# One encoder layer with SSD and windowed attention on one core: the order of work in the SSD forward pass

## The chip, the cores and the metric

The kernel runs on one core of a Trainium2 chip. The metric is the device time of one execution in microseconds. Engines are named TensorE (PE in the rows; PEld is its weight load), VectorE (DVE), ScalarE (ACT), GpSimd (POOL) and SyncE (SP, which here only issues DMAs). Each executes its own queue in order; semaphores hold an instruction until what it reads has been produced.

## The reference

One layer on x of 1024 tokens by 1024 features: RMS norm, one input projection, then two branches. Branch A is a bidirectional state-space scan (SSD) with 16 heads in 2 groups; branch B is windowed attention. Both are gated and normed, concatenated, projected, added to x, and normed. The part that the change touches, for one direction, chunks of 128 tokens:

```python
X = (xh * dt[..., None]).reshape(b, c, CHUNK, SSM_GROUPS, SSM_HPG, SSM_HEAD_DIM)
cs = jnp.cumsum(a, axis=-1)
L = jnp.exp(jnp.where(tril, cs[..., :, None] - cs[..., None, :], -jnp.inf))
CB = jnp.einsum('bclgn,bcsgn->bgcls', Cc, Bc)
y_diag = jnp.einsum('bghcls,bcsghp->bclghp', CB[:, :, None] * L, X)
states = jnp.einsum('bcsgn,bghcs,bcsghp->cbghpn', Bc, jnp.exp(cs[..., -1:] - cs), X)
# carried over the chunks: state = decay * state + states[c]
y_off = jnp.einsum('bclgn,cbghpn,bghcl->bclghp', Cc, states_in, jnp.exp(cs))
...
y = y_fwd + y_bwd + d_skip * xh
y_ssd = rms_norm(y * silu(z), ssd_norm_g)      # per group
```

## The kernel before

All products run on TensorE in 32-bit float; the large projections split each operand into a high and a low part (hi, lo) and take three products. The kernel has these stages: norm of x and transposes; convolution blocks of group 0; the SSD stage of group 0 (backward pass, then forward pass); convolutions of group 1; the SSD stage of group 1; attention, with the output projection fed in between; the rest of the output projection.

Each SSD pass is a loop over 8 chunks. Between its pieces `fill(n)` traces n halves of a projection block, 24 matmuls of 128x512 each (L146), which need nothing from the SSD work. A scheduler orders each engine's queue at build time by a model of the times, so work that was traced later can be placed earlier where its inputs are there.

In a chunk c of a group:

- `weighted(c, d)` (L540): GpSimd makes xd = xk * wst, ScalarE its rounded part xh (L545), VectorE the rest xl (L546).
- `advance(Sold, c, d)` (L549): three TensorE products of Bk with xh, xl, xh into a bank "s" (L552); GpSimd scales the old state by the decay (L557); VectorE adds the two (L558).
- `y_off` (L562): the carried state times CT (L570), times et from DRAM on VectorE (L572).
- Backward pass (L575): `y_off` into yo, which GpSimd's DMA adds to yb_d in DRAM (L579), `advance`, `fill(1)`.
- `scores(c)` (L587): loads cb[0] and cb[1] (E and F: the cumulative sums, broadcast, 512 KB each); TensorE product BT x CT (L596) into a bank "t", VectorE multiplies it by two masks into CB (L600). ScalarE adds the bias of each of 8 heads to E (L607), VectorE that of all heads to F (L608), takes the minimum (L609); ScalarE makes M from CB (L612) and exp(E) (L613); VectorE makes CB * dt in F (L614), adds (L616) and multiplies (L617). M is traced one chunk ahead.
- Forward pass (L621): `y_off` into yb, which a DMA issued by GpSimd accumulates with yb_d (L630); `fill`; the diagonal product of xk and M into the one bank "y" (L635); VectorE adds it to yb (L637); `advance`; then the gating: zt is loaded, GpSimd multiplies (yg, L643), SP's DMA stores yg to y_d (L644), ScalarE squares (L646), GpSimd adds parts (L647, L649) into sqs, which `add_sums` (L514) sums by TensorE (L519).

Buffers in the pool sp are 2 per tag where nothing else is said; xh and xl have 1, yo and yb share 3. PSUM has 3 banks "mm", 2 "t", 2 "s", 1 "y".

Of the kernel before, what the change touches and what calls it, by code (L numbers as in the profile page):

```python
# [10 lines left out]
F32 = mybir.dt.float32  # L11
# [5 lines left out]
P = 128  # L17
S = 1024
# [17 lines left out]
def kernel(  # L36
# [430 lines left out]
    def fill(n):  # L467
        while n:
            if next(left) is None:
                n -= 1  # L470
# [4 lines left out]
    def hb(t, d, c, g):  # L475
        return t[:, d, c, g * HPG:(g + 1) * HPG]

    def bc(t, n):
        return t.unsqueeze(2).broadcast_to([P, HPG, n])

    def v3(t):
        return t.rearrange("p (h d) -> p h d", h=HPG)
# [40 lines left out]
    for g in range(NG):  # L523
# [12 lines left out]
        if g == NG - 1:  # L536
            cpc.close()
            kv_pools.append(pool(ctx, "kvp", side="left"))

        def weighted(c, d):  # L540
            xd = sp.tile([P, 512], F32, tag="xd", name="xd")
            G.tensor_tensor(out=v3(xd), in0=v3(xk[:, c, :]), in1=bc(hb(wst, d, c, g), 64), op=ALU.mult)
            xh = sp.tile([P, 512], F32R, tag="xh", name="xh", bufs=1)
            xl = sp.tile([P, 512], F32R, tag="xl", name="xl", bufs=1)
            A.activation(out=xh, in_=xd, func=AF.Copy)  # L545
            V.tensor_tensor(out=xl, in0=xd, in1=xh.bitcast(F32), op=ALU.subtract)  # L546
            return xh, xl, xh

        def advance(Sold, c, d):  # L549
            ps = bank("s")  # L550
            for i, (b, x) in enumerate(zip((Bk[0], Bk[0], Bk[1]), weighted(c, d))):
                T.matmul(ps, lhsT=b[:, c, :], rhs=x, start=i == 0, stop=i == 2)  # L552
            Sn = sp.tile([P, 512], F32, tag="S", name=f"S{d}")
            if Sold is None:
                A.activation(out=Sn, in_=ps, func=AF.Copy)
            else:
                G.tensor_tensor(out=v3(Sn), in0=v3(Sold), in1=bc(hb(dec, d, c, g), 64), op=ALU.mult)  # L557
                V.tensor_tensor(out=Sn, in0=Sn, in1=ps, op=ALU.add)  # L558
            return Sn

# [14 lines left out]
        for c in range(NSB - 1, -1, -1):  # L575
            if Sb is not None:
                yo = sp.tile([P, 512], F32, tag="yo", name="yo", bufs=3)
                y_off(Sb, c, 1, yo)
                G.dma_start(out=yb_d[g, c], in_=yo, accum_op=ALU.add)  # L579
            if c > 0:  # L580
                Sb = advance(Sb, c, 1)
            if c == 5 and sums:
                add_sums()
            fill(1)
        Sf = None

        def scores(c):  # L587
            cb = []
            for d in range(2):
                t = sp.tile([P, HPG, P], F32, tag=f"cb{d}", name=f"cb{d}", bufs=2)  # L590
                r = cs_d[d, c * NH + g * HPG:c * NH + (g + 1) * HPG, :]
                nc.sync.dma_start(out=t.rearrange("p h l -> p (h l)"),
                                  in_=bass.AP(tensor=r.tensor, offset=r.offset, ap=[[0, P], [1, HPG * P]]))
                cb.append(t)
            ps = bank("t")
            T.matmul(ps[:, 0:P], lhsT=BT[:, c * P:(c + 1) * P], rhs=CT[:, c * P:(c + 1) * P],  # L596
                     start=True, stop=True)
            CB = sp.tile([P, 2, P], F32, tag="CB", name="CB")
            for d in range(2):
                V.tensor_tensor(out=CB[:, d, :], in0=ps[:, 0:P], in1=msk[:, d, :], op=ALU.mult)  # L600


            E, F = cb
            M = sp.tile([P, HPG, P], F32, tag="M", name="M")
            for h in range(HPG):
                hh = g * HPG + h
                A.activation(out=E[:, h, :], in_=E[:, h, :], func=AF.Identity, bias=ncs[:, 0, c, hh:hh + 1])  # L607
            V.tensor_tensor(out=F, in0=F, in1=bc(hb(ncs, 1, c, g), P), op=ALU.add)  # L608
            V.tensor_tensor(out=E, in0=E, in1=F, op=ALU.min)  # L609
            for h in range(HPG):  # L610
                hh = g * HPG + h
                A.activation(out=M[:, h, :], in_=CB[:, 0, :], func=AF.Copy, scale=dt[:, 0, c, hh:hh + 1])  # L612
            A.activation(out=E, in_=E, func=AF.Exp)  # L613
            V.tensor_tensor(out=F, in0=CB[:, 1, :].unsqueeze(1).broadcast_to([P, HPG, P]),  # L614
                            in1=bc(hb(dt, 1, c, g), P), op=ALU.mult)
            V.tensor_tensor(out=M, in0=M, in1=F, op=ALU.add)  # L616
            V.tensor_tensor(out=M, in0=M, in1=E, op=ALU.mult)  # L617
            return M

        Mn = scores(0)  # L620
        for c in range(NSB):  # L621
            M = Mn
            if c < NSB - 1:
                Mn = scores(c + 1)
            yb = sp.tile([P, 512], F32, tag="yo", name="yb", bufs=3)
            if Sf is None:
                nc.sync.dma_start(out=yb, in_=yb_d[g, c])
            else:
                y_off(Sf, c, 0, yb)
                G.dma_start(out=yb, in_=yb_d[g, c], accum_op=ALU.add)  # L630
            fill(FORWARD[c][0])
            py = bank("y")
            for h in range(HPG):
                a = h % 2 * 64
                T.matmul(py[a:a + 64, h // 2 * P:(h // 2 + 1) * P], lhsT=xk[:, c, h * 64:(h + 1) * 64],  # L635
                         rhs=M[:, h, :], start=True, stop=True)
            V.tensor_tensor(out=yb, in0=py, in1=yb, op=ALU.add)  # L637
            if c < NSB - 1:
                Sf = advance(Sf, c, 0)
            zt = sp.tile([P, 4, P], F32, tag="zt", name="zt", bufs=1)  # L640
            nc.sync.dma_start(out=zt, in_=z_d[g * 4:(g + 1) * 4, :, c * P:(c + 1) * P].rearrange("b p s -> p b s"))
            yg = sp.tile([P, 512], F32, tag="yg", name="yg", bufs=1)
            G.tensor_tensor(out=yg, in0=yb, in1=zt.rearrange("p b s -> p (b s)"), op=ALU.mult)  # L643
            nc.sync.dma_start(out=y_d[g, c], in_=yg)  # L644
            y2 = sp.tile([P, 512], F32, tag="y2", name="y2", bufs=1)
            A.activation(out=y2, in_=yg, func=AF.Square)  # L646
            G.tensor_tensor(out=y2[:, 0:256], in0=y2[:, 0:256], in1=y2[:, 256:512], op=ALU.add)  # L647
            sqs = sp.tile([P, P], F32, tag="sqs", name="sqs", bufs=6)
            G.tensor_tensor(out=sqs, in0=y2[:, 0:P], in1=y2[:, P:256], op=ALU.add)  # L649
            sums.append((g, c, sqs))  # L650
            if c == 5:
                add_sums()
            if g == NG - 1 and c == 4:
                load_kv(0, 0)
                load_q(0, 0)
                load_q(0, 1)
            fill(FORWARD[c][1])
    add_sums()
    ssd.close()

# [400 lines left out]
```

## Time and profile before

| | |
|---|---|
| median of 3 runs | 908.02 us (901.15 to 909.67) |
| profiled execution, its own time | 900.58 us |
| its span, first to last instruction | 898.8 us |
| TensorE busy | 848.2 us (94%) |
| VectorE busy | 569.2 us (63%) |
| ScalarE busy | 491.3 us (55%) |
| GpSimd busy | 356.6 us (40%) |
| mean granted TensorE clock | 0.989 |
| mean DMA traffic | 172 GB/s |

Busy time is the time in which an instruction of that engine was under way. Matmuls are pipelined, so their durations overlap; the time of a run of them is read from the starts. The SSD stage of group 0 lies at about 147 to 289 us of the span, that of group 1 at about 407 to 538 us.

### The profile page before, as it was taken

What the parts mean: (1) busy time and instruction counts of PE and PEld (TensorE: products, weight loads), DVE (VectorE), ACT (ScalarE), POOL (GpSimd) and SP (SyncE); (2) the same over time, 40 slices, a digit from 0 to 9 for tenths busy, and PEclk for the clock granted to TensorE, in tenths of its full rate; (3) what the DMA queues carried; (4) which work ended last, traced back from release to release, by engine and by line L of the source; (5) the groups of instructions that cost most, each with busy time, mean ns of one, the idle gap of its engine ahead of it and who ended that gap; (6) DMA issues with size and microseconds to landing.
All of it is one profiled execution on the core that took longest, in us unless ns stands there. A gap on an engine that the chain in (4) does not pass through costs nothing. (4 is left out here: it accounts for less than half of the span.)

```text
span 898.8 us, 13352 instructions
## 1 busy us (share of the span) xinstructions
PE 848.2 (94%) x4622; PEld 714.6 (80%) x4622; DVE 569.2 (63%) x971; ACT 491.3 (55%) x1118; POOL 356.6 (40%) x327
## 2 busy tenths in 40 slices
PE   3999999998898999999979999999999999899997
PEld 2999788886677888888857787887888888688786
DVE  4575766596898375446769945655766767555433
ACT  4642474353656345523645725788867866764222
POOL 3300012533865201134358552273653741735622
PEclk9999999999999999999998999999999999999999
DMA  8122473576788513477859869869856757424421
GB/s 296 75 83 59 155 222 128 141 222 187 223 234 256 166 47 94 117 206 177 261 131 253 225 190 246 243 200 308 245 149 182 221 131 190 145 56 136 132 87 47
DMA packets 127408, 154.25 MB, mean 172 GB/s; under 512 B 42331, under 2 KB 79899, under 8 KB 127212
## 3 DMA queue, kind: packets, MB, share of 16 engines
q1 hardware_dynamic: 121420, 141.35, 51.4%
q0 software_dynamic: 5776, 11.79, 7.4%
q8 instruction: 36, 0.59, 0.3%
q14 instruction: 32, 0.26, 0.1%
q10 hardware_dynamic: 144, 0.26, 0.1%
HBM read 111.58 MB, written 43.88 MB: 173 GB/s over the span
## 5 line engine op out<-in xcount | busy, mean ns | idle before, releaser
L146 PE MATMUL mm<-hhi,whi 128*128 128x512 f32 (+1 forms) x640 | 247.2, 389 | 1.8 <-ACT hhi L224 1.8
L146 PE MATMUL mm<-hlo,whi 128*128 128x512 f32 (+1 forms) x640 | 246.9, 387 | 0.0
L146 PE MATMUL mm<-hhi,wlo 128*128 128x512 f32 (+1 forms) x640 | 246.5, 386 | 0.0
L146 PEld LDWEIGHTS mm<-hhi,whi 128*128 128x128 f32 x640 | 121.6, 191 | 23.5 <-ACT hhi L224 2.5
L146 PEld LDWEIGHTS mm<-hlo,whi 128*128 128x128 f32 x640 | 121.9, 191 | 22.5 <-issue 1.7
L146 PEld LDWEIGHTS mm<-hhi,wlo 128*128 128x128 f32 x640 | 121.9, 191 | 21.7 <-issue 0.7
L695 PE MATMUL mm<-hhi,yl 128*128 128x512 f32 (+1 forms) x264 | 104.8, 397 | 0.8 <-POOL yl L687 0.8
L695 PE MATMUL mm<-hhi,yh 128*128 128x512 f32 (+1 forms) x264 | 104.7, 397 | 0.0
L695 PE MATMUL mm<-hlo,yh 128*128 128x512 f32 (+1 forms) x264 | 104.6, 396 | 0.0
L880 DVE CUSTOM_DVE_ANT_0 lg<-s,bias,nsnk 128x320 f32<-128x320 f32 (+2 forms) x128 | 64.6, 521 | 43.5 <-PE s L877 42.6
L883 ACT ACTIVATE lg<-lg,nm 128x320 f32<-128x320 f32 (+2 forms) x128 | 68.5, 535 | 18.3 <-DVE nm L880 16.4
L250 DVE SCALAR_TENSOR_TENSOR acc<-pad,prm_sb,acc 128x1024 f32<-128x1024 f32 x48 | 62.1, 1301 | 24.4 <-ACT acc L247 23.1
L687 POOL TENSOR_TENSOR yl<-y,yh 128x512 fp32r<-128x512 f32 x32 | 41.8, 1306 | 82.6 <-ACT yh L686 63.8
L134 ACT ACTIVATE whi<-wraw 128x1024 fp32r<-128x1024 f32 x38 | 40.0, 1054 | 41.9 <-PE mm L146 38.1
L137 POOL TENSOR_TENSOR wlo<-wraw,whi 128x1024 fp32r<-128x1024 f32 x12 | 30.2, 2518 | 69.0 <-ACT whi L134 69.0
L695 PEld LDWEIGHTS mm<-hhi,yl 128*128 128x128 f32 x264 | 50.2, 190 | 7.0 <-POOL yl L687 1.2
L607 ACT ACTIVATE cb<-cb,ncs 128x128 f32<-128x128 f32 x128 | 39.4, 390 | 29.8 <-DMA cb<-cs_d 29.8
L695 PEld LDWEIGHTS mm<-hhi,yh 128*128 128x128 f32 x264 | 50.3, 190 | 5.6
L695 PEld LDWEIGHTS mm<-hlo,yh 128*128 128x128 f32 x264 | 50.1, 190 | 5.5
L897 DVE TENSOR_TENSOR pl<-t,ph 128x512 fp32r<-128x512 f32 (+1 forms) x64 | 40.6, 654 | 18.7 <-ACT ph L896 18.0
L435 POOL TENSOR_TENSOR hlo<-oraw,hhi 128x512 fp32r<-128x512 f32 x32 | 41.0, 1292 | 26.6 <-ACT hhi L434 24.7
L137 DVE TENSOR_TENSOR wlo<-wraw,whi 128x1024 fp32r<-128x1024 f32 x26 | 33.7, 1297 | 24.0 <-ACT whi L134 21.4
(233 smaller groups left out, 1749.8 us busy)
## 6 DMA issues: line engine op xcount, KB each, us to landing
wraw<-in_w_blk_dram SPq DMA_DIRECT2D x38, 512.0 KB, 4.2
cb<-cs_d SPq DMA_DIRECT2D x32, 512.0 KB, 5.8
qt<-q_d SPq DMA_DIRECT2D x32, 256.0 KB, 3.8
oraw<-in_w_out_dram SPq DMA_DIRECT2D x32, 256.0 KB, 4.0
et<-es_d SPq DMA_DIRECT2D x56, 128.0 KB, 4.9
yb_d<-pad SPq DMA_DIRECT2D x8, 512.0 KB, 3.9
z_d<-gz SPq DMA_DIRECT2D x16, 256.0 KB, 3.8
zt<-z_d SPq DMA_DIRECT2D x16, 256.0 KB, 3.7
```

The source lines that it names most:

```text
L134: A.activation(out=hi, in_=raw, func=AF.Copy)
L137: eng.tensor_tensor(out=lo, in0=raw, in1=hi.bitcast(F32), op=ALU.subtract)
L146: yield T.matmul(ps, lhsT=l[:, kb, :], rhs=r[sh][:, kb, cols], start=(n == 0), stop=(n == 3 * NKB - 1))
L250: V.scalar_tensor_tensor(out=acc, in0=pad[:, k:k + S], scalar=cw[:, blk * 6 + k:blk * 6 + k + 1], in1=acc, op0=ALU.mult, op1=ALU.add)
L435: G.tensor_tensor(out=lo[:, c:c + 512], in0=raw, in1=hi[:, c:c + 512].bitcast(F32), op=ALU.subtract)
L607: A.activation(out=E[:, h, :], in_=E[:, h, :], func=AF.Identity, bias=ncs[:, 0, c, hh:hh + 1])
L687: G.tensor_tensor(out=lo, in0=t, in1=hi.bitcast(F32), op=ALU.subtract)
L695: yield T.matmul(ps[:, cols], lhsT=l[:, j * P:(j + 1) * P], rhs=r[:, dh * 512 + cols.start:dh * 512 + cols.stop], start=first and n == 0, ...
L880: V.tensor_tensor_reduce(out=l, in0=ps[:, d0 - c0:d1 - c0], in1=bias[:, hp, d0 - f0:d1 - f0], scale=-1.0, scalar=nsnk[:, sk], op0=ALU.add, ...
L883: A.activation(out=l, in_=l, func=AF.Exp, scale=-1.0, bias=nm, accum_out=sm)
L897: V.tensor_tensor(out=pl[0:w, 0:n], in0=ps[0:w, 0:n], in1=ph[0:w, 0:n].bitcast(F32), op=ALU.subtract)
```

## The change

In the SSD stage:

- GpSimd's instructions of a group are chained in the order in which they are traced (`ordered`), its accumulating DMAs among them. Splits of projection weights on GpSimd are not in the chain.
- xd has 1 buffer, xh and xl 2.
- In `advance` the scaling of the old state is traced ahead of the product, and the weighted x can be handed in.
- CB stays in PSUM, in columns 128 to 383 of the bank that holds its product.
- The bias of F is added by ScalarE, one instruction per head.
- In the forward pass `advance` stands ahead of the diagonal product, with xw of the chunk made in the previous one. The accumulating DMA stands behind the addition of the diagonal product. The gating (`finish`, `reduce`) is that of the previous chunk, and y_d is stored from ScalarE's queue.

```diff
+        last = [None]
+
+        def ordered(trace):
+            with ExitStack() as st:
+                if last[0] is not None:
+                    st.enter_context(tc.issue_after(last[0].ins))
+                last[0] = trace()
+
         def weighted(c, d):
-            xd = sp.tile([P, 512], F32, tag="xd", name="xd")
-            G.tensor_tensor(out=v3(xd), in0=v3(xk[:, c, :]), in1=bc(hb(wst, d, c, g), 64), op=ALU.mult)
-            xh = sp.tile([P, 512], F32R, tag="xh", name="xh", bufs=1)
-            xl = sp.tile([P, 512], F32R, tag="xl", name="xl", bufs=1)
+            xd = sp.tile([P, 512], F32, tag="xd", name="xd", bufs=1)
+            ordered(lambda: G.tensor_tensor(out=v3(xd), in0=v3(xk[:, c, :]), in1=bc(hb(wst, d, c, g), 64), op=ALU.mult))
+            xh = sp.tile([P, 512], F32R, tag="xh", name="xh")
+            xl = sp.tile([P, 512], F32R, tag="xl", name="xl")
...
-        def advance(Sold, c, d):
+        def advance(Sold, c, d, xw=None):
+            Sn = sp.tile([P, 512], F32, tag="S", name=f"S{d}")
+            if Sold is not None:
+                ordered(lambda: G.tensor_tensor(out=v3(Sn), in0=v3(Sold), in1=bc(hb(dec, d, c, g), 64), op=ALU.mult))
             ps = bank("s")
-            for i, (b, x) in enumerate(zip((Bk[0], Bk[0], Bk[1]), weighted(c, d))):
+            for i, (b, x) in enumerate(zip((Bk[0], Bk[0], Bk[1]), xw or weighted(c, d))):
...
-                G.dma_start(out=yb_d[g, c], in_=yo, accum_op=ALU.add)
+                ordered(lambda: G.dma_start(out=yb_d[g, c], in_=yo, accum_op=ALU.add))
...
-            CB = sp.tile([P, 2, P], F32, tag="CB", name="CB")
+            CB = ps[:, P:3 * P].rearrange("p (d l) -> p d l", d=2)
...
-            V.tensor_tensor(out=F, in0=F, in1=bc(hb(ncs, 1, c, g), P), op=ALU.add)
+                A.activation(out=F[:, h, :], in_=F[:, h, :], func=AF.Identity, bias=ncs[:, 1, c, hh:hh + 1])
...
+        def finish(c, yb):
+            zt = sp.tile([P, 4, P], F32, tag="zt", name="zt", bufs=1)
+            nc.sync.dma_start(out=zt, in_=z_d[g * 4:(g + 1) * 4, :, c * P:(c + 1) * P].rearrange("b p s -> p b s"))
+            yg = sp.tile([P, 512], F32, tag="yg", name="yg", bufs=1)
+            ordered(lambda: G.tensor_tensor(out=yg, in0=yb, in1=zt.rearrange("p b s -> p (b s)"), op=ALU.mult))
+            y2 = sp.tile([P, 512], F32, tag="y2", name="y2", bufs=1)
+            A.activation(out=y2, in_=yg, func=AF.Square)
+            nc.scalar.dma_start(out=y_d[g, c], in_=yg)
+            return y2
+
+        def reduce(c, y2):
+            ordered(lambda: G.tensor_tensor(out=y2[:, 0:256], in0=y2[:, 0:256], in1=y2[:, 256:512], op=ALU.add))
+            sqs = sp.tile([P, P], F32, tag="sqs", name="sqs", bufs=6)
+            ordered(lambda: G.tensor_tensor(out=sqs, in0=y2[:, 0:P], in1=y2[:, P:256], op=ALU.add))
+            sums.append((g, c, sqs))
 
-        Mn = scores(0)
+        Mn, xw, ready = scores(0), weighted(0, 0), None
         for c in range(NSB):
             M = Mn
             if c < NSB - 1:
                 Mn = scores(c + 1)
             yb = sp.tile([P, 512], F32, tag="yo", name="yb", bufs=3)
-            if Sf is None:
-                nc.sync.dma_start(out=yb, in_=yb_d[g, c])
-            else:
+            first = Sf is None
+            if not first:
                 y_off(Sf, c, 0, yb)
-                G.dma_start(out=yb, in_=yb_d[g, c], accum_op=ALU.add)
+            if c < NSB - 1:
+                Sf = advance(Sf, c, 0, xw)
+            y2 = finish(*ready) if ready else None
+            if c < NSB - 2:
+                xw = weighted(c + 1, 0)
+            if y2 is not None:
+                reduce(c - 1, y2)
             fill(FORWARD[c][0])
             py = bank("y")
...
-            V.tensor_tensor(out=yb, in0=py, in1=yb, op=ALU.add)
-            if c < NSB - 1:
-                Sf = advance(Sf, c, 0)
...
+            if first:
+                V.tensor_copy(yb, py)
+            else:
+                V.tensor_tensor(out=yb, in0=py, in1=yb, op=ALU.add)
+            ordered(lambda: G.dma_start(out=yb, in_=yb_d[g, c], accum_op=ALU.add))
+            ready = c, yb
...
+    reduce(NSB - 1, finish(*ready))
     add_sums()
```

(The last addition stands inside the loop over the groups, after the loop over the chunks.)

## Rows read from the trace of the kernel before

**Rows 1.** Stretches, backward and forward pass of each group: busy us, clock, DMA.

```profile
core 0: us, PE busy (x) PEld busy (x) DVE busy (x) ACT busy (x) POOL busy (x), PEclk, DMA share, GB/s
147.00:213.00 66.00, 66.00 (x332) 54.90 (x331) 46.80 (x56) 32.17 (x75) 27.72 (x26) 1.00 0.60 165
213.00:289.00 76.00, 66.59 (x389) 52.89 (x388) 63.60 (x70) 42.51 (x103) 48.05 (x38) 0.98 0.79 234
407.00:444.00 37.00, 37.00 (x197) 30.67 (x195) 29.22 (x35) 19.73 (x52) 14.00 (x12) 1.00 0.84 214
444.00:538.00 94.00, 83.94 (x466) 67.48 (x464) 67.33 (x79) 45.99 (x109) 54.95 (x45) 0.96 0.74 208
```

**Rows 2.** Waits of TensorE in the span: us in total, times, longest us.

```profile
PE y L635 <- DVE yb L637: 6.2, 3, 2.4
PE s L552 <- DVE xl L546: 5.7, 5, 2.2
PE s L570 <- DVE S L558: 4.9, 5, 2.1
...
PE y L635 <- DVE M L617: 1.9, 1, 1.9
...
PE t L519 <- POOL sqs L649: 0.5, 1, 0.5
```

**Rows 3.** VectorE in order of time: start, us, instruction, idle before and releaser.

```profile
223.88 0.69 DVE L637 TENSOR_TENSOR yb<-y,yb 128x512 f32<-128x512 f32 x1 [5.07 <-DMA yb<-yb_d]
...
240.47 1.23 DVE L608 TENSOR_TENSOR cb<-cb,ncs 128x1024 f32<-128x1024 f32 x1 [1.44 <-DMA cb<-cs_d]
241.61 0.68 DVE L558 TENSOR_TENSOR S<-S,s 128x512 f32<-128x512 f32 x1
```

**Rows 4.** DMA issues: queue, count, KB each, median us to landing.

```profile
yb<-yb_d POOLq DMA_DIRECT2D x14, 256.0 KB, 5.7
```

**Rows 5.** Stretches of 10 us, columns as in group 1.

```profile
240.00:250.00 10.00, 7.90 (x32) 6.27 (x31) 9.53 (x11) 6.67 (x19) 6.68 (x7) 0.83 0.71 217
470.00:480.00 10.00, 7.32 (x36) 6.08 (x37) 9.72 (x9) 4.08 (x11) 9.22 (x7) 0.66 0.64 170
```

**Rows 6.** GpSimd in order of time, a step of the backward pass.

```profile
160.86 0.99 POOL L579 DMA_DIRECT2D yb_d<-yo  x1 [3.52 <-DVE yo L572]
161.56 1.38 POOL L557 TENSOR_TENSOR S<-S,dec 128x512 f32<-128x512 f32 x1
162.82 1.11 POOL L542 TENSOR_TENSOR xd<-xk,wst 128x512 f32<-128x512 f32 x1
```

**Rows 7.** Groups by line and form, 147 to 545 us: busy us, mean ns, idle before.

```profile
L546 DVE TENSOR_TENSOR xl<-xd,xh 128x512 fp32r<-128x512 f32 x28 | 29.5, 1054 | 7.6 <-ACT xh L545 7.6
...
L614 DVE TENSOR_TENSOR cb<-CB,dt 128x1024 f32<-128x1024 f32 x16 | 23.4, 1470 | 0.1
...
L608 DVE TENSOR_TENSOR cb<-cb,ncs 128x1024 f32<-128x1024 f32 x14 | 19.7, 1409 | 11.0 <-DMA cb<-cs_d 11.0
...
L545 ACT ACTIVATE xh<-xd 128x512 fp32r<-128x512 f32 x28 | 17.5, 625 | 29.9 <-DVE yo L572 12.8 <-PE s L552 9.4 <-issue 5.0
...
L572 DVE TENSOR_TENSOR yo<-s,et 128x512 f32<-128x512 f32 x14 | 9.6, 685 | 15.9 <-PE s L570 15.9
...
L555 ACT ACTIVATE S<-s 128x512 f32<-128x512 f32 x4 | 2.3, 581 | 3.5 <-PE s L552 3.5
```

**Rows 8.** ScalarE in order of time, the bias of one E.

```profile
192.96 2.46 ACT L607 ACTIVATE cb<-cb,ncs 128x128 f32<-128x128 f32 x8 [2.39 <-DMA cb<-cs_d]
```

**Rows 9.** The one DMA issued by ScalarE: duration ns min/median/max.

```profile
L779 ACTq DMA_DIRECT2D out_dram<-acc x1: 371/371/371, 895.0 to 895.0; - x1
```

**Rows 10.** TensorE in order of time, steps of the first backward pass.

```profile
158.77 1.05 PE L570 MATMUL s<-CT,S 128*128 128x128 f32 x8
...
159.89 0.39 PE L552 MATMUL s<-xl,Bk 128*128 128x512 f32 x1
...
178.86 1.05 PE L570 MATMUL s<-CT,S 128*128 128x128 f32 x8
...
187.73 1.05 PE L570 MATMUL s<-CT,S 128*128 128x128 f32 x8
```

More of the change, by code (lines that the diff above doesn't have):

```diff
@@ L547, in weighted @@
             return xh, xl, xh
-        def advance(Sold, c, d):
+        def advance(Sold, c, d, xw=None):
+            Sn = sp.tile([P, 512], F32, tag="S", name=f"S{d}")
+            if Sold is not None:
+                ordered(lambda: G.tensor_tensor(out=v3(Sn), in0=v3(Sold), in1=bc(hb(dec, d, c, g), 64), op=ALU.mult))
             ps = bank("s")
-            for i, (b, x) in enumerate(zip((Bk[0], Bk[0], Bk[1]), weighted(c, d))):
+            for i, (b, x) in enumerate(zip((Bk[0], Bk[0], Bk[1]), xw or weighted(c, d))):
                 T.matmul(ps, lhsT=b[:, c, :], rhs=x, start=i == 0, stop=i == 2)
-            Sn = sp.tile([P, 512], F32, tag="S", name=f"S{d}")
             if Sold is None:
@@ L556, in advance @@
             else:
-                G.tensor_tensor(out=v3(Sn), in0=v3(Sold), in1=bc(hb(dec, d, c, g), 64), op=ALU.mult)
                 V.tensor_tensor(out=Sn, in0=Sn, in1=ps, op=ALU.add)
@@ L636 @@
                          rhs=M[:, h, :], start=True, stop=True)
-            V.tensor_tensor(out=yb, in0=py, in1=yb, op=ALU.add)
-            if c < NSB - 1:
-                Sf = advance(Sf, c, 0)
[L640 to L650, printed above, removed]
+            if first:
[4 more added lines that the diff above has]
+            ready = c, yb
             if c == 5:
```

## The prediction

> **What bounds the kernel now.** I read the stretches first. In the four stretches that cover the SSD stage of both head groups [rows 1] TensorE is the full one: 66.0 of 66 us and 37.0 of 37 us while the backward passes run, but only 66.6 of 76 us and 83.9 of 94 us in the forward passes. So TensorE sets the time, and what this change can win directly is its idle time there: 9.4 + 10.1 = 19.5 us. VectorE is the next engine: 63.6 of 76 us in the first forward pass, ScalarE 42.5 and GpSimd 48.1.
>
> Then the waits of TensorE [rows 2], which name that idle time. 6.2 us: the product L635 waits for VectorE's addition L637, because there is one "y" bank and L637 has to empty it. 5.7 us: the state product L552 waits for the split xl. 4.9 us: the carried state's product L570 waits for the addition L558. 1.9 us: L635 waits for the weights M. 0.5 us: for sqs. These are 19.2 of the 19.5 us.
>
> Then VectorE's order of time at two of these places [rows 3], to see why it was late. At 223.88 it had stood 5.07 us for a DMA: L637 reads yb, and yb is first accumulated from DRAM, which takes 5.7 us from issue to landing [rows 4]. At 240.47 it had stood 1.44 us for the broadcast load cb, and did L608 (1.23 us), before it could do L558, for which TensorE waited. VectorE executes in order, so a late transfer at its head holds back work that has nothing to do with it.
>
> Last the clock [rows 5]: it was granted at 0.83 and 0.66 on average over two stretches of 10 us, which contain times at the lower level (1.2 GHz). In both TensorE had idled, 2.1 and 2.7 us of the 10. The lost clock is 0.17 x 10 + 0.34 x 10 = 5.1 us.
>
> **The change part by part.**
>
> *Gating a chunk behind.* L637 no longer reads what a DMA brings; the addition is made first and the accumulate transfer is issued after it, by GpSimd. The 6.2 us at L635 go. The first chunk swaps a load on SP for one more accumulate on GpSimd (2 in all, 0.99 us each by [rows 6]), and an addition for a copy of the same size. The wait for the landing (5.7 us) moves to GpSimd's yg, with xd of the next chunk, two reductions and the next accumulate queued behind it. xd feeds the state product of the next chunk; a forward pass of 76 us has 8 chunks, 9.5 us each, so landing, yg and xd fit, with little over. The wait for sqs (0.5 us) goes, because its producer is a chunk older. After the last chunk the gating starts 5.7 us later; the projections' matmuls of the same program point cover it. Zero taken; 5.7 us if they don't.
>
> *Next state and weighted x ahead.* In the forward pass xd, xh and xl of a chunk are made a chunk before the product that reads them, and the state's product and addition come ahead of the diagonal product. This aims at the 5.7 and the 4.9 us. Two buffers of xh and xl (one before) lift the wait for the previous product. I take off 2.5 us of the 10.6 as left over, since GpSimd's order can still be late.
>
> *Score bias.* 16 VectorE instructions L608 go (1.41 us each on average [rows 7], 22.5 us), and with them VectorE's standing for cb. ScalarE gets 128 more instructions: 8 take 2.46 us [rows 8], so 16 x 2.46 = 39 us. In the forward passes ScalarE rises from 42.5 by at most 8 x 2.46 = 19.7 to 62 us in a stretch that has at least 66.6 us of TensorE work: full but not the bound. Behind ScalarE's wait for cb now stand xh and the projections' evictions; three "mm" banks cover these. The chain to M grows: the two biases ran side by side, now one after the other, 2.46 - 1.41 = 1.05 us at least and 2.46 us at most, for 14 chunks (the first of each group has the backward pass ahead of it): 15 to 34 us uncovered, 0 covered. Its cover is that M is made a chunk ahead, and M delayed TensorE once, by 1.9 us [rows 2]. So I take 2.5 us, near the covered end.
>
> A rule speaks against this part. The row: eight instructions of 128x128 take 2.46 us, where one of 128x1024 took 1.41 on VectorE. The Trainium skill, Perfetto Trace Analysis, Optimizing Scalar/DVE Operations, says that each instruction pays an access overhead that depends on the memory (about 93 ns for ScalarE on SBUF, 51 on PSUM), so that on a saturated engine larger operations are better. By it 128 x 93 ns = 12 us of the added time (an estimate from that page) are overhead; the sum by the row stays.
>
> *CB left in PSUM.* ScalarE's 128 copies L612 now read PSUM. Nearest rows: 128x512 from PSUM 581 ns, from SBUF 625 [rows 7], so 0 to 44 ns less each. VectorE's writing of CB to PSUM is not in the trace; L572, which reads PSUM, costs the same 685 ns as an unstretched operation of its size, so I take no change. The "t" bank is held longer, two banks for two chunks in flight, with nothing else but add_sums using them here: zero.
>
> *y_d stored from ScalarE's queue.* SP loses a wait for yg, ScalarE issues 16 DMAs (0.37 us each at the only such row [rows 9]): 6 us in all, off the path.
>
> *GpSimd in a fixed order.* In the forward pass this is what the parts above need. In the backward pass it costs. Today xd runs ahead of the state; in the order written it stands behind the accumulate of its own chunk (which waits for yo) and the state's scaling. From the start of L570 at 158.77 to the end of xd at 163.93 [rows 6, 10] is 5.16 us; with xh 0.63, xl 1.05, the last product 0.39, and the addition 0.69 (the size of L572) the chain of a step becomes 7.92 us [rows 7, 10]. The steps at 158.77 to 178.86 took 20.09 / 3 = 6.70 us, all TensorE work. Uncovered that is 1.22 us in 12 steps: 14.6 us. The cover is projection matmuls pulled forward: the step from 178.86 to 187.73 took 8.87 us with TensorE never idle (66.0 of 66). So between 0 and 14.6; I take 3, nearer to the row that shows the cover.
>
> **The sum.** Gains: 6.2 + (10.6 - 2.5) + 0.5 = 14.8 us, and half of the clock, 2.5: 17.3. Losses: M 2.5, backward steps 3: 5.5. Net 11.8 us. The profiled execution took 900.6 us (span 898.8 and 1.8 around it): 888.8 for one like it. It lies 7.4 us below the median of the three runs, 908.0; the sum is a difference, so on the median it gives 896.2.
>
> **The rivals.**
>
> *All waits go.* ScalarE and GpSimd keep up, TensorE is never idle and keeps its clock: 908.0 - 19.5 - 5.1 = 883.4. For it: VectorE, busy for 130.9 us in the two forward stretches, loses most of 22.5 us and its long waits. Against it: VectorE and GpSimd stretch each other; L614 with both inputs in SBUF took 1.47 us on average, L546 1.05, while L572, with one input in PSUM, took 0.685 for half the size of L614. The Trainium skill, SBUF — State Buffer, Who interferes with whom, says that a VectorE instruction with two SBUF inputs contends with a GpSimd one that reads SBUF, and one with at most one doesn't; by it L614, whose CB is now in PSUM, falls from 1.47 to twice 0.685, 1.6 us over 16, which favours this case slightly. These rows agree with it.
>
> *The scores take the place.* Forward waits go but M becomes late, at the lower end 1.05 us in 14 chunks, 14.7 us where I took 2.5: 896.2 + 12.2 = 908.4, no change. For it: ScalarE already idles for cb, and now everything on it stands behind two such loads. Against it: one wait for M in 16 chunks.
>
> *The backward order costs more than the forward pass wins (slower).* One mechanism: xd behind the accumulate of its chunk, at every step. The rest of the sum is a gain of 14.8, so it decides where a step is 14.8 / 12 = 1.23 us longer than today and uncovered: at the bare chain of 7.92 us. With one more microsecond a step of queueing, about one L614 ahead of yo or xl, it costs 12 x 2.22 = 26.6 us: 908.0 - 14.8 + 26.6 = 919.8. For it: the links pass three in-order engines that have other work. Against it: the step of 8.87 us without idle time.
>
> *It doesn't do what it says.* If the state still arrives late because GpSimd's scaling stands behind an accumulate, the 10.6 us stay: 896.2 + 8.1 = 904.3, again no change.
>
> **How the numbers follow.** Forecast 896.2, chance 0.47, its own range 889 to 903 (the low end with nothing left over, the whole clock and 2 us less for M and the backward steps; the high end the reverse). All waits gone 0.12. Scores or a state still late 0.22 together. Slower 0.19. The range reaches from 884 to 919: outside lie about half of the first rival and two thirds of the slower one, 0.06 + 0.13. A measurement of this kernel tells about 1%, 9 us, from no change. Faster (below 899): 0.38 of the forecast's 0.47 and the 0.12, 0.50. Slower (above 917): most of 0.19 and a part of the late scores, 0.22. The same: 0.28.
>
> **What would show it.** Right: TensorE's wait for the addition after L635 is gone, the waits of both state products fall below 3 us in all, GpSimd waits for yb instead of VectorE, VectorE has no wait for cb, and no stretch below full clock in the two forward passes. Wrong: TensorE waits for xl in the backward passes (the fixed order), or for M before most diagonal products (ScalarE), or the first attention logits come late.

## The result, and the profile after

The kernel became slower: 963.1 us (median of 4 runs, 958.2 to 965.7) against 907.3 us, a ratio of 1.063 with a 95% interval of 1.059 to 1.067. The profiled execution took 961.7 us (span 959.9) where that of before took 900.6 (898.8): 61.1 us more.

From the page of the changed kernel, busy times over the span, and the granted TensorE clock in 40 slices, in tenths:

```profile
PE 874.7 (91%) x4622; PEld 732.1 (76%) x4622; DVE 558.1 (58%) x955; ACT 524.2 (55%) x1246; POOL 349.8 (36%) x329
PEclk9999999999999598999999666899999999999999
```

TensorE has the same 4622 matmuls as before. It was busy for 874.7 us, 26.5 more than before, and idle for 959.9 - 874.7 = 85.2 us, 34.6 more. These two make the 61.1 us. The busy time grew mostly because matmuls ran at the lower clock level: the mean granted clock is 0.95 where it was 0.989. An estimate from the busy time and the granted clock of every 5 us of both traces puts the busy time lost to the clock at 31 us, before at 7, so 23 of the 26.5.

Stretches of the changed kernel, columns as in [rows 1]: backward and forward pass of group 0, then of group 1.

```profile
152.00:276.00 124.00, 123.87 (x587) 102.48 (x586) 53.08 (x66) 50.52 (x114) 28.93 (x23) 1.00 0.52 148
276.00:355.00 79.00, 68.15 (x365) 53.14 (x363) 68.14 (x66) 52.59 (x141) 49.82 (x42) 0.85 0.62 175
409.00:519.00 110.00, 110.00 (x527) 91.34 (x526) 52.00 (x65) 46.41 (x109) 24.96 (x21) 1.00 0.67 175
519.00:602.00 83.00, 46.21 (x243) 34.55 (x242) 48.66 (x60) 37.62 (x109) 45.52 (x49) 0.69 0.61 159
```

The backward passes still look perfect: TensorE is full at full clock. But they last 124 and 110 us, before 66 and 60. (For group 1 [rows 1] shows 37, because its stretch starts at 407 us, after two of the seven products L570 of that pass, at 393.46 and 400.52. With them it starts at about 384, as in the second table below.) The forward pass of group 1 has 36.8 us without TensorE work (before 10.1) and a clock of 0.69. The same stretches, of the projection's matmuls L146 alone (busy and count of PE, of PEld, clock, DMA), first of the changed kernel, then of the kernel before:

```profile
152.00:276.00 124.00, 115.33 (x484) 89.75 (x483) 1.00 0.52 148
276.00:355.00 79.00, 37.08 (x154) 28.31 (x152) 0.85 0.62 175
409.00:519.00 110.00, 101.08 (x424) 78.52 (x423) 1.00 0.67 175
519.00:602.00 83.00, 4.93 (x19) 3.16 (x17) 0.69 0.61 159
```

```profile
147.00:213.00 66.00, 54.28 (x226) 41.85 (x225) 1.00 0.60 165
213.00:289.00 76.00, 47.86 (x189) 35.49 (x188) 0.98 0.79 234
384.00:444.00 60.00, 48.30 (x203) 37.23 (x201) 1.00 0.80 205
444.00:538.00 94.00, 62.74 (x251) 47.11 (x251) 0.96 0.74 208
```

This is the result in two tables. The two backward passes now hold 484 + 424 of these matmuls, before 226 + 203; the forward passes are left with 154 + 19, before 189 + 251. The convolution stage between the groups is left with 189 (355 to 409 us), before 396 (289 to 384). The supply was used up early, and the last forward pass had almost none left to do while it waited.

Waits of TensorE after (us in total, times, longest us), which answer [rows 2]:

```profile
PE t L519 <- POOL sqs L643: 15.1, 5, 7.9
...
PE s L580 <- DVE S L568: 8.1, 4, 3.2
PE s L564 <- ACT xh L554: 8.0, 6, 2.3
PE mm L146 <- ACT pad L245: 6.8, 2, 5.6
PE y L666 <- DVE M L627: 4.9, 3, 3.2
```

In the new numbering L580 is the carried state's product, L564 the state's, L666 the diagonal one, L568 the state's addition, L643 the sums of squares. None of these waits lies in a backward pass, although the cause does.

One backward step of the changed kernel in order of time (start, us, instruction, idle before and releaser), TensorE, then GpSimd, ScalarE and VectorE, which answers [rows 6, 10]:

```profile
238.66 1.05 PE L580 MATMUL s<-CT,S 128*128 128x128 f32 x8
248.68 0.39 PE L564 MATMUL s<-xh,Bk 128*128 128x512 f32 x1
...
255.34 1.05 PE L580 MATMUL s<-CT,S 128*128 128x128 f32 x8
...
240.75 0.88 POOL L589 DMA_DIRECT2D yb_d<-yo  x1 [1.76 <-DVE yo L582]
241.34 1.37 POOL L561 TENSOR_TENSOR S<-S,dec 128x512 f32<-128x512 f32 x1
242.34 1.36 POOL L551 TENSOR_TENSOR xd<-xk,wst 128x512 f32<-128x512 f32 x1
...
243.74 0.63 ACT L554 ACTIVATE xh<-xd 128x512 fp32r<-128x512 f32 x1 [1.07 <-POOL xd L551]
...
244.40 0.69 DVE L555 TENSOR_TENSOR xl<-xd,xh 128x512 fp32r<-128x512 f32 x1 [1.01 <-ACT xh L554]
250.27 0.69 DVE L568 TENSOR_TENSOR S<-S,s 128x512 f32<-128x512 f32 x1
```

The step takes 255.34 - 238.66 = 16.7 us; in [rows 10] it took 6.7. The chain is the one forecast: yo, the accumulate's issue, the scaling, xd, xh, xl. It is done at 245.1, 6.4 us after L580. TensorE reaches the product only at 248.68, and the next L580 4.4 us after the addition, because its queue, laid out at build time, has projection matmuls there: 66 of them in this step, 65 to 84 in the others, where one `fill` traces 24.

### The profile page after: what moved, and what is told of

The parts are those of the page before. It is cut to its first block, busy times and chain, and to the rows that moved or that the text cites. A ratio compares the mean times of both kernels' runs of the same rounds, so it can differ in the third digit from the quotient of the medians.

```text
span 959.9 us, 13463 instructions
## 1 busy us (share of the span) xinstructions
PE 874.7 (91%) x4622; PEld 732.1 (76%) x4622; DVE 558.1 (58%) x955; ACT 524.2 (55%) x1246; POOL 349.8 (36%) x329
## 5 line engine op out<-in xcount | busy, mean ns | idle before, releaser
L146 PE MATMUL mm<-hhi,whi 128*128 128x512 f32 (+1 forms) x640 | 248.3, 390 | 8.7 <-ACT pad L245 6.8
L146 PE MATMUL mm<-hlo,whi 128*128 128x512 f32 (+1 forms) x640 | 247.4, 388 | 0.0
L146 PE MATMUL mm<-hhi,wlo 128*128 128x512 f32 (+1 forms) x640 | 247.0, 387 | 0.0
L146 PEld LDWEIGHTS mm<-hhi,whi 128*128 128x128 f32 x640 | 122.1, 192 | 31.0 <-ACT pad L245 7.5
L146 PEld LDWEIGHTS mm<-hlo,whi 128*128 128x128 f32 x640 | 122.5, 192 | 22.2 <-issue 0.9
L146 PEld LDWEIGHTS mm<-hhi,wlo 128*128 128x128 f32 x640 | 122.2, 191 | 21.6 <-issue 0.3
L250 DVE SCALAR_TENSOR_TENSOR acc<-pad,prm_sb,acc 128x1024 f32<-128x1024 f32 x48 | 72.1, 1509 | 17.4 <-ACT acc L247 16.5
L137 DVE TENSOR_TENSOR wlo<-wraw,whi 128x1024 fp32r<-128x1024 f32 x26 | 38.3, 1472 | 34.3 <-ACT whi L134 34.3
L589 POOL DMA_DIRECT2D yb_d<-yo x14 | 12.5, 892 | 119.6 <-DVE yo L582 72.2
L435 POOL TENSOR_TENSOR hlo<-oraw,hhi 128x512 fp32r<-128x512 f32 x32 | 41.0, 1291 | 26.6 <-ACT hhi L434 25.6
```

The costliest lines, as they stand in the source:

```text
L137: eng.tensor_tensor(out=lo, in0=raw, in1=hi.bitcast(F32), op=ALU.subtract)
L146: yield T.matmul(ps, lhsT=l[:, kb, :], rhs=r[sh][:, kb, cols], start=(n == 0), stop=(n == 3 * NKB - 1))
L250: V.scalar_tensor_tensor(out=acc, in0=pad[:, k:k + S], scalar=cw[:, blk * 6 + k:blk * 6 + k + 1], in1=acc, op0=ALU.mult, op1=ALU.add)
L435: G.tensor_tensor(out=lo[:, c:c + 512], in0=raw, in1=hi[:, c:c + 512].bitcast(F32), op=ALU.subtract)
L589: ordered(lambda: G.dma_start(out=yb_d[g, c], in_=yo, accum_op=ALU.add))
```

## Experiments

Every kernel below computes the whole result. Ratios are to the kernel before, measured beside it on the same chip; brackets are 95% intervals.

**Where the 61 us come from.** Theory A: GpSimd's order in the backward pass, which puts xd behind its own chunk's accumulate. Theory B: the forward pass, with the bias on ScalarE. Theory C: the single buffer of xd. The first kernel is the changed one without the chain in the backward pass:

```diff
-        last = [None]
+        last, fixed = [None], [False]
...
-                if last[0] is not None:
+                if last[0] is not None and fixed[0]:
...
+        fixed[0] = True
         Mn, xw, ready = scores(0), weighted(0, 0), None
```

> The changed kernel, but GpSimd's instructions of the backward pass are not chained; the forward pass keeps its fixed order. Theory A (the fixed order of the backward pass puts xd behind the accumulate of its own chunk, so a step of the state takes 16.7 us instead of 6.7, and the projection matmuls that are pulled in front of it are missing in the forward pass): the steps of the backward pass are back to 7 to 9 us, the forward passes again hold 150 or more projection matmuls each, and the time is 885 to 910 us. Theory B (the forward pass itself, with ScalarE's second bias and GpSimd waiting for the landing of yb, is what got slower): stays above 940 us. Theory C (one buffer of xd instead of two keeps xd from running ahead): stays above 940 us, with steps of 16 us.

Measured: 901.5 us, 0.998 [0.996, 1.000]. Releasing that order gives back nearly everything (1.063 to 0.998, 59 us); xd has one buffer here too, so C falls, and the forward pass is as changed, so B falls. Waits of TensorE in the SSD stage of this kernel:

```profile
PE s L564 <- ACT xh L554: 6.4, 5, 2.1
...
PE s L564 <- DVE xl L555: 4.6, 4, 2.4
PE s L580 <- DVE S L568: 2.6, 2, 2.1
```

The second keeps the order everywhere but traces the backward weighted x a chunk ahead, as the forward pass does:

```diff
-        Sb = None
+        Sb, xw = None, weighted(NSB - 1, 1)
         for c in range(NSB - 1, -1, -1):
+            xn = weighted(c - 1, 1) if c > 1 else None
...
-                Sb = advance(Sb, c, 1)
+                Sb = advance(Sb, c, 1, xw)
+            xw = xn
```

> The changed kernel with its fixed order everywhere, but the weighted x of the backward pass is traced one chunk ahead too, so that xd stands in front of the accumulate of the chunk that uses it. Theory A: it is not that the order is fixed but where xd stands in it; steps of 7 to 9 us, time 885 to 910 us. Theory B: above 940 us. Theory C (one buffer of xd): above 930 us.

Measured: 906.1 us, 1.001 [0.999, 1.003]. So it is not the fixed order as such, but xd's place in it. The backward steps of this kernel took 9.0 to 12.0 us, more than the 7 to 9 expected, and yet the time is that of before: its forward passes still have 180 and 194 projection matmuls (230 to 300 and 465 to 550 us). A longer, covered step costs little as long as the supply lasts.

The third is the kernel before with that order alone: only the backward accumulate, scaling and xd are chained, with two buffers for xd. (For this the scaling is also traced ahead of the product, as in the change; the fourth kernel, the changed one without any order, has that too.)

```diff
...
-            G.tensor_tensor(out=v3(xd), in0=v3(xk[:, c, :]), in1=bc(hb(wst, d, c, g), 64), op=ALU.mult)
+            f = lambda: G.tensor_tensor(out=v3(xd), in0=v3(xk[:, c, :]), in1=bc(hb(wst, d, c, g), 64), op=ALU.mult)
+            ordered(f) if d else f()
...
+            if Sold is not None and d:
+                ordered(lambda: G.tensor_tensor(out=v3(Sn), in0=v3(Sold), in1=bc(hb(dec, d, c, g), 64), op=ALU.mult))
...
-                G.dma_start(out=yb_d[g, c], in_=yo, accum_op=ALU.add)
+                ordered(lambda: G.dma_start(out=yb_d[g, c], in_=yo, accum_op=ALU.add))
```

> The kernel before, with one thing added: in the backward pass GpSimd's accumulate, scaling of the state and xd are chained in that order, as in the changed kernel. Everything else is as before, two buffers of xd among it. Theory A: 940 to 970 us, steps of 15 to 17 us, and forward passes with few projection matmuls. Theories B and C: within 1% of before, 898 to 917 us.

Measured: 949.3 us, 1.049 [1.046, 1.052]. One edit, in neither the scores nor the forward pass, costs 44 us. Two stretches of it, columns as in [rows 1], in the backward and in the forward pass of group 0:

```profile
150.00:250.00 100.00, 100.00 (x473) 82.12 (x472) 57.24 (x64) 38.81 (x83) 22.04 (x18) 1.00 0.51 153
...
290.00:360.00 70.00, 51.97 (x285) 40.81 (x282) 66.66 (x62) 41.48 (x93) 38.83 (x34) 0.88 0.63 180
```

The same picture: no idle time where the order was set, 18 us of it one pass later.

The fourth takes all chaining away (`issue_after` deleted from `ordered`):

> The changed kernel without any chaining on GpSimd; state, weighted x and gating are traced as in the change, ScalarE does the bias, CB stays in PSUM. Theory A: 880 to 905 us, and the difference to the kernel with the backward pass freed shows what the forward pass's fixed order costs or gives, between -10 and +10 us. Theory B: above 930 us. Theory C: above 930 us.

Measured: 905.9 us, 1.001 [0.998, 1.004]. That is a microsecond outside the 880 to 905 expected. The order of the forward pass, which the other parts were to need, is worth little: 905.9 without, 901.5 with it, and the two intervals overlap.

**What became of the forward gains.** The second kernel of this pair is the kernel before with the bias of F on ScalarE alone; the first is e1 with that bias back on VectorE:

```diff
-                A.activation(out=F[:, h, :], in_=F[:, h, :], func=AF.Identity, bias=ncs[:, 1, c, hh:hh + 1])
+            V.tensor_tensor(out=F, in0=F, in1=bc(hb(ncs, 1, c, g), P), op=ALU.add)
```

> The changed kernel with GpSimd's order fixed in the forward pass only, and the score bias of F again one VectorE instruction per chunk. Theory D (with the backward order out of the way, ScalarE's 39 us of new bias work take back what the forward pass wins: TensorE waited 6.4 us for xh from ScalarE in the kernel with the backward pass freed): faster than that kernel by 5 us or more, 885 to 897 us, waits for xh under 2 us. Theory E (the bias is a wash, what is left are misses of an order made at build time): 897 to 910 us, TensorE's wait moves from xh to VectorE's xl or S.

> The kernel before with one thing changed: the score bias of F by ScalarE per head. The forecast held it nearly free (2.5 us lost for later M, and VectorE no longer standing for cb). Theory D: 5 us or more slower than before, 910 to 925 us. Theory E: within 1% of before, 896 to 914 us.

Measured: 899.1 us, 0.992 [0.990, 0.995], and 906.2 us, 1.001 [0.999, 1.003]. Alone the bias costs nothing that can be told, as theory E expected; beside the other changes it costs about 0.6% (0.998 against 0.992). Waits of TensorE in e5:

```profile
PE s L564 <- ACT xh L554: 7.8, 5, 2.3
```

The wait for xh did not go with ScalarE's load, against theory D, so that load is not its cause; nor did it move to xl or S, against theory E. GpSimd of the same kernel in order of time shows what is:

```profile
257.74 2.15 POOL L634 TENSOR_TENSOR yg<-yb,zt 128x512 f32<-128x512 f32 x1 [4.53 <-DMA yb<-yb_d]
259.85 2.02 POOL L551 TENSOR_TENSOR xd<-xk,wst 128x512 f32<-128x512 f32 x1
```

xd of the next chunk stands behind yg, and yg behind the landing of yb. So the next kernel traces xd ahead of the gating (theory F: the wait goes and is won; theory G: what stands behind is late next):

```diff
                 Sf = advance(Sf, c, 0, xw)
-            y2 = finish(*ready) if ready else None
             if c < NSB - 2:
                 xw = weighted(c + 1, 0)
+            y2 = finish(*ready) if ready else None
```

> As the kernel with the bias back on VectorE and the backward pass unchained, and in the forward pass's fixed order the weighted x of the next chunk stands ahead of the gating of the chunk behind, so that it doesn't wait behind yg for the landing of yb. Theory F (what the forward pass still loses is xd queued behind that landing: TensorE waits 7.8 us for xh): the waits for xh fall under 2 us, 888 to 897 us. Theory G (the order made at build time misses somewhere else as soon as one wait is gone): within 0.5% of the kernel with the bias back, 895 to 904 us, other waits of the same sum.

Measured: 897.0 us, 0.991 [0.988, 0.995], the lowest median here, though not clear of e5's 0.992. Its waits of TensorE:

```profile
PE s L580 <- DVE S L568: 7.6, 4, 4.0
...
PE s L564 <- ACT xh L554: 0.9, 1, 0.9
```

Both theories hold in part: 7.8 us for xh became 0.9, and 7.6 us for the state came in their place.

**Is it the queue or the chain?** In the changed kernel the chain was done while TensorE still had matmuls queued ahead of the product. So perhaps only the queue was wrong (A1). The next kernel holds the matmuls of a step behind the previous step's state product (and those of the forward pass behind the last of the backward pass); the one after does the same to e2, whose weighted x is ahead:

```diff
-                T.matmul(ps, lhsT=b[:, c, :], rhs=x, start=i == 0, stop=i == 2)
+                product[0] = T.matmul(ps, lhsT=b[:, c, :], rhs=x, start=i == 0, stop=i == 2)
...
+        def fill_behind(n):
+            with ExitStack() as st:
+                if held[0] is not None:
+                    st.enter_context(tc.issue_after(held[0].ins))
+                fill(n)
...
-            fill(1)
+            fill_behind(1)
+            held[0] = product[0]
...
```

> The changed kernel with GpSimd's order as it is, but TensorE's projection matmuls of a backward step may not be placed ahead of the state product of the step before, and those of the forward pass not ahead of the backward pass's last state product. So each step keeps 24 projection matmuls. Theory A1 (the chain of about 8 us costs little by itself, the loss comes from 40 to 66 projection matmuls being queued into each step, which starves the forward pass): steps of 8 to 10 us, 1 to 2.5 us of idle TensorE in each of 12 steps, forward passes with 200 or more projection matmuls, 895 to 930 us. Theory A2 (the longer chain of the state itself is the loss, wherever the matmuls stand): above 940 us.

> The same hold on the projection matmuls, and the weighted x of the backward pass one chunk ahead in GpSimd's fixed order. Theory A1: backward steps of about 7 us with TensorE hardly idle and forward passes that keep their matmuls; faster than the kernel with the hold alone by 5 to 20 us, 880 to 905 us. Theory A2: about 905 us, as without the hold.

Measured: 1013.3 us, 1.118 [1.115, 1.121], and 921.3 us, 1.017 [1.011, 1.024]. Waits of TensorE in the first of them:

```profile
PE s L564 <- ACT xh L554: 54.4, 13, 7.1
PE t L262 <- DVE cv L254: 20.4, 3, 13.6
```

With 3 matmuls ahead of the product and 21 behind, TensorE stands about 4 us a step for xh. A1 in this form fell: the time lies in A2's range. But the hold is no clean test: the matmuls held back also starved the convolution stage (L262), in e8 too (19.9 us), whose time lies above both ranges.

A milder hold, on e9: projection halves at most four state products ahead, and at most three (`past[-4]` or `past[-3]` in place of `held[0]`).

> The same, and a projection half may be placed ahead of at most 4 state products that were traced before it, so that the matmuls are spread more evenly, but the convolutions ahead still get theirs. If what is left is a lack of matmuls at the end of the forward passes: 2 to 8 us faster than without the hold, 883 to 895 us. If the idle time only moves: within 0.5% of it.

> The same with at most 3. More even still, less for the convolutions ahead: expected between 3 us faster and 8 us slower than with 4, because holding the matmuls with 1 left TensorE idle for 19.9 us ahead of the transposes of cv.

Measured: 903.7 us, 0.996 [0.994, 0.997], and 899.1 us, 0.991 [0.988, 0.994]. Neither beats e9's 897.0: without the long chain these two holds win nothing. (The second was expected at most 3 us faster than the first; it was 4.6 us faster.)

The changed kernel with the 24 matmuls of a step held behind its L580, three halves of each group free:

```diff
+            if c < 5:
+                held[0] = off[0]
+            fill_behind(1)
...
```

> The changed kernel with GpSimd's order as it is, and the 24 projection matmuls of a backward step held behind the first product of the step (L580), so that they stand where the long chain runs; three of the eight halves are free for the stage ahead. Theory A3 (the chain of the changed order takes about 8 us and costs 1 to 2.5 us a step where 24 matmuls of 5.5 us stand in it; the rest of the 56 us is that the queue built around it holds two to three times as many): steps of 8 to 10 us in the backward pass, 912 to 940 us. Theory A2 (the chain itself is the loss): above 945 us.

Measured: 961.2 us, 1.059 [1.056, 1.062]. The later steps fell to 8.2 to 8.8 us, with about 1 us of waiting for the state in each (13.0 us in 13); the first ones, now without matmuls, waited 23.8 us for xh. The time lies in A2's range, but the test is not conclusive: the free halves took the matmuls away from the first steps and moved the loss there.

Last an even dealing: three halves in the first backward chunk of a group, one in each later one, held behind the first product of its step, and two fewer in the forward pass, held behind the backward pass's last state product; once with the backward order (e12), once with e1's release of it (e13). Theory A2: the longer chain costs 40 us or more however the matmuls are dealt; A3: most of the loss was the dealing, and 10 to 18 us are left between the two.

```diff
-    FORWARD = ((1, 1), (1, 1), (0, 1), (1, 1), (1, 1), (0, 1), (1, 1), (1, 1))
+    FORWARD = ((0, 1), (1, 1), (0, 1), (1, 1), (0, 1), (0, 1), (1, 1), (1, 1))
...
-            fill(1)
+            held[0] = off[0]
+            fill_behind(3 if c == NSB - 1 else 1)
...
```

> The changed kernel with GpSimd's order as it is and the projection halves dealt out evenly: three at the first chunk of a backward pass, then one in each step, held behind the first product of the step, and two fewer in the forward pass. Theory A3 (the longer chain costs about 1 us of idle TensorE a step where 24 matmuls stand in it; what cost 56 us was the number of matmuls that the build placed in each step and that the forward pass then lacked): steps of 8 to 9 us all through the backward passes, idle TensorE of about 1 us in each, forward passes with little idle time, 905 to 930 us. Theory A2 (the longer chain is the loss, however the matmuls stand): above 945 us.

> The same dealing of the projection halves with GpSimd's backward pass unchained. It is the control: the difference between the two is the price of the backward order when the matmuls are dealt evenly. Theory A3: 10 to 18 us less than the kernel with the order (12 to 14 steps of about 1 us), 890 to 915 us. Theory A2: 40 us or more less.

Measured: 941.1 us, 1.038 [1.034, 1.042], and 898.9 us, 0.994 [0.991, 0.997]: 42 us apart. The difference is what A2 expected (40 or more) and far above A3's 10 to 18; e12's own time lies between the two ranges. So with this dealing the order costs 42 us. None of the dealings tried (e7, e11, e12) brings the kernel with this order below 941 us; that no other could is not shown. From the first to the seventh of the products that open the steps (L588 in these two kernels) e12 takes 67.3 us in group 0 and 70.0 in group 1, e13 47.1 and 47.3: the whole difference lies there. A stretch in the backward pass of group 0, columns as in [rows 1], of e12, then of e13:

```profile
150.00:250.00 100.00, 83.55 (x376) 64.94 (x376) 50.86 (x64) 43.54 (x111) 34.05 (x34) 0.89 0.51 136
```

```profile
150.00:250.00 100.00, 98.23 (x497) 80.58 (x498) 63.49 (x76) 58.82 (x155) 48.65 (x45) 0.95 0.69 187
```

With the matmuls dealt evenly the loss stands where it is made: 16.5 us idle in this stretch against 1.8. Steps of e13 take 7.0 to 7.3 us after the first. In e12 the last two of each group take 8.2 and 8.7, the earlier ones 10.7 to 16.7 in group 0 and 11.3 to 18.3 in group 1. TensorE in the first step of group 0 and at both ends of the 8.2 us step, then GpSimd and ScalarE in the first step:

```profile
155.82 2.08 PE L588 MATMUL s<-CT,S 128*128 128x128 f32 x8 [0.15 <-ACT S L566]
169.04 0.79 PE L564 MATMUL s<-xh,Bk 128*128 128x512 f32 x1 [3.79 <-ACT xh L554]
172.53 2.05 PE L588 MATMUL s<-CT,S 128*128 128x128 f32 x8 [1.55 <-DVE S L568]
...
206.18 1.13 PE L588 MATMUL s<-CT,S 128*128 128x128 f32 x8 [1.41 <-DVE S L568]
...
214.39 1.13 PE L588 MATMUL s<-CT,S 128*128 128x128 f32 x8 [0.87 <-DVE S L568]
...
162.48 1.37 POOL L551 TENSOR_TENSOR xd<-xk,wst 128x512 f32<-128x512 f32 x1
...
162.41 2.45 ACT L627 ACTIVATE cb<-cb,ncs 128x128 f32<-128x128 f32 x8 [0.43 <-DMA cb<-cs_d]
166.02 2.44 ACT L628 ACTIVATE cb<-cb,ncs 128x128 f32<-128x128 f32 x8 [1.16 <-DMA cb<-cs_d]
168.37 0.62 ACT L554 ACTIVATE xh<-xd 128x512 fp32r<-128x512 f32 x1
```

xd is done at 163.85, but ScalarE executes in order and has 16 biases of the forward pass's scores in its queue, which wait for the broadcast load; xh starts 4.5 us later. Here the chain is long because it passes through an engine that stands for something else.

## Why the prediction was wrong

**The step that failed** is "So between 0 and 14.6; I take 3, nearer to the row that shows the cover", the cost of the backward order. Two things were wrong in it; a third, the length of the bare chain, was nearly right.

*The cover was taken as free.* The 8.87 us step without idle time [rows 10] was real, and so was the cover: no backward pass of the changed kernel has idle time. But projection matmuls that cover a longer chain are taken from a later stage. The sum should have counted them: 212 more (1081 against 869) lie in the four passes of after, at 0.226 us each (two successive ones on TensorE before, at 187.04 and 187.27, stand about that far apart) 48 us of work. The passes take 396 us instead of 296, so 396 - 296 - 48 = 52 us were lost in them, most of the 61. The sign that the forecast gave for this failure, TensorE waiting for xl in the backward passes, did not show: it waits for nothing there.

*The bare chain was nearly right.* The 8.2 us step of e12, which nothing else disturbs, has 5.11 us from the product that opens it to the end of xd (forecast 5.16), 0.66 for xh, 0.72 for xl (forecast 1.05), 0.85 for the three products (forecast one, 0.39), 0.73 for the addition and 0.14 to the next product: 8.21 us, where 7.92 was forecast. Over 12 steps the 0.3 us make 3.5. The changed kernel's step took 16.7 us all the same.

*It was no upper bound.* The 14.6 assumed that each engine takes its link of the chain at once. In the step of the changed kernel shown above xl was done after 6.4 us and the product came after 10.0, behind 40 projection matmuls; e12 shows 4.5 us at ScalarE alone in one step. The price of the order was 44 us alone (e3) and 42 us with matmuls dealt evenly (e12 against e13), about three times the 14.6.

The slower rival had the mechanism, "xd behind the accumulate of its chunk", and the point from which it decides. Its price of 26.6 us allowed one microsecond of queueing a step; e3's 44 us is far above that too. It deserved more than 0.19: the deciding point was the bare chain itself.

**The forward gain, point by point** (e1 has it without the backward loss).

- *The 6.2 us at the diagonal product*: right as to the mechanism. In e1 TensorE has no wait left at this product. VectorE no longer waits for yb; GpSimd does, as forecast, 60.4 us in 15 times in e1 and 47.4 in the changed kernel. VectorE's waits for the load of cb are gone too, but in their place it waits 28.7 us for ScalarE's two biases (e1).
- *State and weighted x*: the 10.6 us were forecast to leave 2.5. In e1 13.6 us of such waits are left (6.4 + 4.6 + 2.6). "Landing, yg and xd fit, with little over" was the weak sentence: they fit on average, but xd is not done when the product is due. e9 shows that xd ahead of the gating removes the wait for xh and brings a wait for the state.
- *The clock*: no gain with e1 (mean 0.986 in the profiled execution, before 0.989); only e9 has it (0.993).
- *The bias*: 2.5 us forecast; nothing alone (e6), 5 to 6 us in company (e5 against e1). The rival of late scores had a small part.
- *CB in PSUM*: VectorE's product of CB and dt took 1.22 us, before 1.47 [rows 7]. It took 1.22 in e1 as well, and 1.63 in e6, where ScalarE has the same bias but CB lies in SBUF. The Trainium skill, SBUF — State Buffer, Who interferes with whom, pointed this way; the trace agrees.
- *The end*: "Zero taken; 5.7 us if they don't" (the last gating uncovered). The changed kernel paid 13.9 us there. GpSimd at the last two chunks, and TensorE's wait for it:

```profile
588.80 1.25 POOL L634 TENSOR_TENSOR yg<-yb,zt 128x512 f32<-128x512 f32 x1 [3.73 <-DMA yb<-yb_d]
...
591.99 0.88 POOL L672 DMA_DIRECT2D yb<-yb_d  x1
597.26 1.25 POOL L634 TENSOR_TENSOR yg<-yb,zt 128x512 f32<-128x512 f32 x1 [4.39 <-DMA yb<-yb_d]
...
592.10 0.59 PE L519 MATMUL t<-ones,sqs 128*128 128x1 f32 x2 [6.00 <-POOL sqs L643]
600.56 0.59 PE L519 MATMUL t<-ones,sqs 128*128 128x1 f32 x2 [7.88 <-POOL sqs L643]
```

In GpSimd's fixed order the last accumulate is issued behind the gating of the chunk before, so two landings come one after the other. In e13 this wait is 0.7 us, and e1 has none: with matmuls left over it is hidden. It is the same supply again.

So the 14.8 + 2.5 us of forward gains were worth 2 us as written (e1) and 8 us in the best arrangement (e9: 897.0, within a microsecond of the forecast 896.2, but of another kernel).

**What stays open.** Why the build lays 65 to 84 projection matmuls into a backward step of the changed kernel, 40 of them in the step shown ahead of a product that the chip could have started sooner. And, of the difference between e12 and e13: in their profiled executions 29.7 of 42.8 us are idle time of TensorE and 13.1 longer busy time. How much of the idle time is the longer chain itself, and how much is queueing on ScalarE and VectorE, no run separates.

## What to carry to other kernels

Work that covers a longer chain is not free: count how much of it there is until the last stage that needs it, and look for its absence a stage later, where the profile will show the idle time. Before fixing an engine's order, follow the one operation in it that an otherwise independent chain waits for, and put it ahead of any instruction that waits for late data; here moving that one operation was worth 57 us (e2 against the changed kernel). A busy share of 100% in a stage says nothing on whether the stage became longer.

## What was not expected of the hardware

The cost of idle time came twice. In 519 to 602 us of the changed kernel TensorE was busy for 46 of 83 us and its granted clock was 0.69, so part of the time it was at 1.2 GHz. There eight products of 128x128 took up to 2.08 us, against 1.05 at 2.4 GHz (a stretch of it, columns as in [rows 1], and its product):

```profile
570.00:580.00 10.00, 6.45 (x30) 4.60 (x29) 8.40 (x9) 3.71 (x9) 6.46 (x7) 0.50 0.46 100
...
573.26 2.08 PE L580 MATMUL s<-CT,S 128*128 128x128 f32 x8
```

In 409 to 519 us, busy throughout, the clock was 1.00. Of the 61 us, 34.6 were idle time and 26.5 longer busy time, by the estimate above 23 of it such slower matmuls.
